# Running XOR over 67 million integers: six tile buffers instead of four, a merged carry path, and a descriptor cap

## Chip, cores, metric

One core of a Trainium2 chip. Times are device microseconds of that core. The kernel is a single program that is executed several times; medians are over those executions, and the profile is of one of them. A run counts as slow when it is over 1.5% above the fastest run of the same kernel; with one core this label rests on the time alone.

## The reference

```python
def setup_inputs():
    return {"x": np.random.randint(0, 256, (8192, 8192), dtype=np.int32)}

def reference(x):
    return np.bitwise_xor.accumulate(x.flatten()).reshape(x.shape)   # given back as int64
```

The kernel gets x as int64 and writes int64: 537 MB in and 537 MB out. As the values fit in 8 bits, it computes on the low 32-bit word of each element and leaves the high word alone.

## The kernel before

A tile is 128 partitions x 4096 elements of 8 bytes, 32,768 B a partition, 4 MB in all; 128 tiles. VectorE scans each partition with a tree of XORs in place, with strides. What carries from one partition to the next, and from one tile to the next, goes through TensorE: the 8 bits of each partition's total are multiplied by a triangular matrix of ones, and the lowest bit of each sum is the XOR.

```python
_F_CONFIGS = [(4096, (8, 8, 8, 8)), ...]
_NB = 4                                   # tile buffers
...
def front(i):                             # VectorE
    dve.wait_ge(sem_in[b], 16 * (i // NB + 1))     # the load has landed
    up_sweep(tb)                          # 28 XORs: 7 of 128x512, 7 of 128x64, 7 of 128x8, 7 of 128x1
    # mvi = total & 1<<k for 8 bits; mvf = mvi as float

def tail(i):
    dve.wait_ge(sem_pe, i + 1)
    # cint = psC as int; rint = cint & maskint; rfbuf = rint as float
    # ebuf = sum(rfbuf); tb[:, 0:1] = ebuf          (what this partition starts from)
    cd(lambda: dve.tensor_copy(c2int.ap(), psC2[0:1, q * _NMV : (q + 1) * _NMV]))
    cd(lambda: dve.tensor_tensor(gint.ap(), c2int.ap(), maskint[0:1, :], ALU.bitwise_and))
    cd(lambda: dve.tensor_copy(gmask[0:1, nq * _NMV : (nq + 1) * _NMV], gint.ap()))
    down_sweep(tb)                        # XORs of 8, 56, 448 and 3584 elements a partition

for i in range(T):
    front(i)
    if i > 0:
        tail(i - 1)
tail(T - 1)

# TensorE, tile i, after tail(i-1):
pe.matmul(psC[:, ...],    lmat,            mvf, start=True,  stop=False)
pe.matmul(psC[:, ...],    onesrow,         gmask, start=False, stop=True)
pe.matmul(psC2[0:1, ...], onescol,         mvf, start=True,  stop=False)   # one output row
pe.matmul(psC2[0:1, ...], onesrow[0:1,0:1], gmask, start=False, stop=True)

# SyncE issues the loads, ScalarE the stores:
if use > 0: sp.wait_ge(sem_out[b], 16 * use)      # the buffer's last store has landed
sp.dma_start(dst, src).then_inc(sem_in[b], 16)
...
act.wait_ge(sem_dve, dve_after_tail[i])
act.dma_start(dst, src).then_inc(sem_out[b], 16)
```

## Time and profile before

| | before |
|---|---|
| time, median of 4 runs | 2707.84 us (2706.84 to 2713.7) |
| span of the profiled run | 2705.8 us |
| VectorE (DVE) busy | 2347.6 us |
| 16 DMA engines, sum of both queues | 96.2% |
| moved | 1074 MB, 397 GB/s |
| VectorE waiting for loads | 148.3 us in 70 waits |

q1 is the load queue, q10 the store queue. The prediction shows these lines and reads them. Two more lines of the kernel before are needed later. First the page's chain that ended last, by engine, then the group of the widest strided sweep (columns: line, engine, operation, shapes, count | busy us, mean ns of one | idle us just before, and what ended it):

```profile
DMA 58%; DVE 39%; issue 2%; DVEq 0%; PE 0%
```

```profile
L156 DVE TENSOR_TENSOR tbuf<-tbuf 128x512 int32<-128x512 int32 x896 | 914.6, 1021 | 180.8 <-DMA tbuf<-in_x_dram 148.3
```

The first says that the end of the program follows from transfers more than from sweeps.

### The profile page before, as it was taken

What the parts mean: (1) busy time and instruction counts of PE and PEld (TensorE: products, weight loads), DVE (VectorE), ACT (ScalarE), POOL (GpSimd) and SP (SyncE); (2) the same over time, 40 slices, a digit from 0 to 9 for tenths busy, and PEclk for the clock granted to TensorE, in tenths of its full rate; (3) what the DMA queues carried; (4) which work ended last, traced back from release to release, by engine and by line L of the source; (5) the groups of instructions that cost most, each with busy time, mean ns of one, the idle gap of its engine ahead of it and who ended that gap; (6) DMA issues with size and microseconds to landing.
All of it is one profiled execution on the core that took longest, in us unless ns stands there. A gap on an engine that the chain in (4) does not pass through costs nothing.

```text
span 2705.8 us, 7983 instructions
## 1 busy us (share of the span) xinstructions
PE 174.7 (6%) x1024; PEld 149.1 (6%) x1024; DVE 2347.6 (87%) x5376; POOL 1.9 (0%) x17
## 2 busy tenths in 40 slices
PE   0000000000000000000000000000000000000000
PEld 0000000000000000000000000000000000000000
DVE  7988888888888888888888888888888888888886
POOL 0000000000000000000000000000000000000000
DMA  8999999999999999999999999999999999999997
GB/s 372 364 399 400 395 408 402 393 407 405 400 393 403 406 391 411 404 397 403 403 404 392 394 405 395 391 404 407 400 394 406 401 392 404 406 401 398 410 395 327
DMA packets 36919, 1074.27 MB, mean 397 GB/s; under 512 B 4097, under 2 KB 4097, under 8 KB 4097
## 3 DMA queue, kind: packets, MB, share of 16 engines
q1 hardware_dynamic: 18432, 536.88, 48.9%
q10 hardware_dynamic: 18432, 536.88, 47.3%
q14 instruction: 47, 0.38, 0.0%
q8 instruction: 8, 0.13, 0.0%
HBM read 536.87 MB, written 536.87 MB: 397 GB/s over the span
## 4 chain that ended last, share of the span: by engine, by line
DMA 58%; DVE 39%; issue 2%; DVEq 0%; PE 0%
DMA out_dram<-tbuf 29%; DMA tbuf<-in_x_dram 29%; DVE tbuf L156 24%; DVE tbuf L175 11%; DVE tbuf L166 0%; DVE mvf L196 0%; DVE rfbuf L218 0%; DVE mvi L188 0%; DVE rint L214 0%; DVE cint L209 0%; DVE ebuf L220 0%; DVE gmask L237 0%; DVE c2int L227 0%; DVE gint L232 0%; DVE tbuf L224 0%
## 5 line engine op out<-in xcount | busy, mean ns | idle before, releaser
L156 DVE TENSOR_TENSOR tbuf<-tbuf 128x512 int32<-128x512 int32 (+3 forms) x3584 | 1459.2, 407 | 273.4 <-DMA tbuf<-in_x_dram 148.3
L175 DVE TENSOR_TENSOR tbuf<-tbuf 128x56 int32<-128x56 int32 (+2 forms) x384 | 658.8, 1716 | 13.2
L257 PE MATMUL psC<-mvf,lmat 128*128 128x8 f32 x256 | 76.3, 372 | 2511.1 <-DVE tbuf L175 2485.2
L257 PEld LDWEIGHTS psC<-mvf,lmat 128*128 128x128 f32 x256 | 64.2, 312 | 2525.2 <-DVE tbuf L175 2499.4
L264 PE MATMUL psC<-gmask,onesrow 1*128 1x8 f32 x256 | 75.8, 367 | 0.0
L264 PEld LDWEIGHTS psC<-gmask,onesrow 1*128 1x128 f32 x256 | 63.7, 308 | 3.1
L209 DVE CAST cint<-psC 128x8 int32<-128x8 f32 x128 | 21.3, 166 | 14.5 <-PE psC L279 1.5
L166 DVE TENSOR_TENSOR tbuf<-tbuf 128x8 int32<-128x8 int32 x128 | 22.1, 173 | 4.4
L218 DVE CAST rfbuf<-rint 128x8 f32<-128x8 int32 x128 | 21.8, 170 | 4.4
L196 DVE CAST mvf<-mvi 128x8 f32<-128x8 int32 x128 | 21.9, 171 | 4.4
L188 DVE TENSOR_TENSOR mvi<-tbuf,maskint 128x8 int32<-128x8 int32 x128 | 21.4, 167 | 4.5
L271 PE MATMUL psC<-mvf,onescol 128*1 128x8 f32 x256 | 25.1, 172 | 0.0
L214 DVE TENSOR_TENSOR rint<-cint,maskint 128x8 int32<-128x8 int32 x128 | 21.3, 166 | 4.4
L279 PE MATMUL psC<-gmask,onesrow 1*1 1x8 f32 x256 | 24.6, 166 | 0.0
L220 DVE TENSOR_REDUCE ebuf<-rfbuf 128x1 f32<-128x8 f32 x128 | 20.6, 161 | 4.4
L237 DVE CAST gmask<-gint 1x8 f32<-1x8 int32 x128 | 20.2, 158 | 4.4
L227 DVE CAST c2int<-psC 1x8 int32<-1x8 f32 x128 | 19.8, 154 | 4.4
L232 DVE TENSOR_TENSOR gint<-c2int,maskint 1x8 int32<-1x8 int32 x128 | 19.7, 154 | 4.4
L224 DVE CAST tbuf<-ebuf 128x1 int32<-128x1 f32 x128 | 19.6, 153 | 4.5
L271 PEld LDWEIGHTS psC<-mvf,onescol 128*1 128x1 f32 x256 | 10.9, 81 | 3.1
L279 PEld LDWEIGHTS psC<-gmask,onesrow 1*1 1x1 f32 x256 | 10.3, 76 | 5.2
L127 POOL MEMSET maskint<- 128x1 int32 x8 | 0.8, 98 | 0.7 <-POOLq L324 0.3
(9 smaller groups left out, 1.3 us busy)
## 6 DMA issues: line engine op xcount, KB each, us to landing
tbuf<-in_x_dram SPq DMA_DIRECT2D x128, 4096.0 KB, 21.8
out_dram<-tbuf ACTq DMA_DIRECT2D x128, 4096.0 KB, 21.1
```

Of the source, the lines that this page charges most:

```text
L156: lambda o=o, i1=i1: dve.tensor_tensor(o, o, i1, ALU.bitwise_xor)
L166: cd(lambda: dve.tensor_tensor(ot, ot, it, ALU.bitwise_xor))
L175: lambda o=o, i1=i1: dve.tensor_tensor(o, o, i1, ALU.bitwise_xor)
L188: lambda: dve.tensor_tensor(mvi[:, q * _NMV : (q + 1) * _NMV], sb, maskint.ap(), ALU.bitwise_and,)
L196: lambda: dve.tensor_copy(mvf[:, q * _NMV : (q + 1) * _NMV], mvi[:, q * _NMV : (q + 1) * _NMV],)
L209: lambda: dve.tensor_copy(cint.ap(), psC[:, q * _NMV : (q + 1) * _NMV])
L214: lambda: dve.tensor_tensor(rint.ap(), cint.ap(), maskint.ap(), ALU.bitwise_and)
L218: cd(lambda: dve.tensor_copy(rfbuf.ap(), rint.ap()))
L257: pe.matmul(psC[:, q * _NMV : (q + 1) * _NMV], lmat.ap(), mvf[:, q * _NMV : (q + 1) * _NMV], start=True, stop=False,)
L264: pe.matmul(psC[:, q * _NMV : (q + 1) * _NMV], onesrow.ap(), gmask[0:1, q * _NMV : (q + 1) * _NMV], start=False, stop=True,)
L271: pe.matmul(psC2[0:1, q * _NMV : (q + 1) * _NMV], onescol.ap(), mvf[:, q * _NMV : (q + 1) * _NMV], start=True, stop=False,)
L279: lambda q=q: pe.matmul(psC2[0:1, q * _NMV : (q + 1) * _NMV], onesrow[0:1, 0:1], gmask[0:1, q * _NMV : (q + 1) * _NMV], start=False, stop= ...
```

## The change

Intent: more buffers, so that loads and stores run further ahead; one copy and one mask for both PSUM results instead of two of each; a cap on the length of a DMA descriptor.

```diff
-    (4096, (8, 8, 8, 8)),
+    (4096, (8, 8, 8, 8), 6),
...
-_NB = 4
+_MAX_DESC_BYTES = 32768
...
-                    dve.wait_ge(sem_pe, i + 1)
-                    cd(lambda: dve.tensor_copy(cint.ap(), psC[:, q * _NMV : (q + 1) * _NMV]))
+                    dve.wait_ge(sem_pe, 2 * (i + 1))
+                    cd(lambda: dve.tensor_copy(cint.ap(), psC[:, pqs]))          # 16 wide now
-                            rint.ap(), cint.ap(), maskint.ap(), ALU.bitwise_and
+                            rint.ap(), cint.ap(), mask16.ap(), ALU.bitwise_and
-                    cd(lambda: dve.tensor_copy(rfbuf.ap(), rint.ap()))
+                    cd(lambda: dve.tensor_copy(rfbuf.ap(), rint[:, 0:_NMV]))
...
-                    (copy of psC2 to c2int, mask of c2int to gint: both gone)
-                            gmask[0:1, nq * _NMV : (nq + 1) * _NMV], gint.ap()
+                            gmask[0:1, nq * _NMV : (nq + 1) * _NMV],
+                            rint[0:1, _NMV : 2 * _NMV],
...
-                        psC2[0:1, q * _NMV : (q + 1) * _NMV],   onescol.ap(),
+                        psC[:, c0 + _NMV : c0 + 2 * _NMV],      onesq.ap(),     # 128 output rows
-                            psC2[0:1, ...],  onesrow[0:1, 0:1],
+                            psC[:, c0 + _NMV : c0 + 2 * _NMV],  onesrow.ap(),
...
-                    sp.dma_start(dst, src).then_inc(sem_in[b], 16)
+                    sp.dma_start(dst, src, max_dma_last_dim=_MAX_DESC_BYTES).then_inc(sem_in[b], 16)
-                    act.dma_start(dst, src).then_inc(sem_out[b], 16)
+                    act.dma_start(dst, src, max_dma_last_dim=_MAX_DESC_BYTES).then_inc(sem_out[b], 16)
```

(The setup of the wider mask and of the square of ones is left out.)

More of the change, by code (lines that the diff above doesn't have):

```diff
@@ L10 @@
 _F_CONFIGS = [
-    (4096, (8, 8, 8, 8)),
-    (2048, (8, 8, 8, 4)),
-    (512, (8, 8, 8)),
-    (256, (4, 4, 4, 4)),
-    (64, (4, 4, 4)),
+    (4096, (8, 8, 8, 8), 6),
+    (2048, (8, 8, 8, 4), 4),
+    (512, (8, 8, 8), 4),
+    (256, (4, 4, 4, 4), 4),
+    (64, (4, 4, 4), 4),
 ]
-_NB = 4
 _NMV = 8
+_MAX_DESC_BYTES = 32768
 class _Chain:
@@ L55, in bass_scan_xor_kernel @@
         out32t = out.tensor
-    F = None
-    RADS = None
-    for f, rads in _F_CONFIGS:
-        if N % (P * f) == 0 and N // (P * f) >= 1:
-            F, RADS = f, rads
+    F = RADS = NB = None
+    for f, rads, nb in _F_CONFIGS:
+        if N % (P * f) == 0:
+            F, RADS, NB = f, rads, nb
             break
@@ L64, in bass_scan_xor_kernel @@
     T = N // (P * F)
-    NB = min(_NB, T)
+    NB = min(NB, T)
     L = len(RADS)
@@ L87, in bass_scan_xor_kernel @@
         ]
-        maskint = es.enter_context(nc.sbuf_tensor("maskint", [P, _NMV], DT.int32))
+        mask16 = es.enter_context(nc.sbuf_tensor("mask16", [P, 2 * _NMV], DT.int32))
         lmat = es.enter_context(nc.sbuf_tensor("lmat", [P, P], DT.float32))
+        onesq = es.enter_context(nc.sbuf_tensor("onesq", [P, P], DT.float32))
         onesrow = es.enter_context(nc.sbuf_tensor("onesrow", [1, P], DT.float32))
-        onescol = es.enter_context(nc.sbuf_tensor("onescol", [P, 1], DT.float32))
         gmask = es.enter_context(nc.sbuf_tensor("gmask", [1, 2 * _NMV], DT.float32))
@@ L94, in bass_scan_xor_kernel @@
         mvf = es.enter_context(nc.sbuf_tensor("mvf", [P, 2 * _NMV], DT.float32))
-        cint = es.enter_context(nc.sbuf_tensor("cint", [P, _NMV], DT.int32))
-        rint = es.enter_context(nc.sbuf_tensor("rint", [P, _NMV], DT.int32))
+        cint = es.enter_context(nc.sbuf_tensor("cint", [P, 2 * _NMV], DT.int32))
+        rint = es.enter_context(nc.sbuf_tensor("rint", [P, 2 * _NMV], DT.int32))
         rfbuf = es.enter_context(nc.sbuf_tensor("rfbuf", [P, _NMV], DT.float32))
         ebuf = es.enter_context(nc.sbuf_tensor("ebuf", [P, 1], DT.float32))
-        c2int = es.enter_context(nc.sbuf_tensor("c2int", [1, _NMV], DT.int32))
-        gint = es.enter_context(nc.sbuf_tensor("gint", [1, _NMV], DT.int32))
-        psC = es.enter_context(nc.psum_tensor("psC", [P, 2 * _NMV], DT.float32))
-        psC2 = es.enter_context(nc.psum_tensor("psC2", [P, 2 * _NMV], DT.float32))
+        psC = es.enter_context(nc.psum_tensor("psC", [P, 4 * _NMV], DT.float32))
         sem_pool = es.enter_context(nc.semaphore("c_pool"))
@@ L106, in bass_scan_xor_kernel @@
         sem_pe = es.enter_context(nc.semaphore("c_pe"))
-        sem_act = es.enter_context(nc.semaphore("c_act"))
-        sem_sp = es.enter_context(nc.semaphore("c_sp"))
         sem_in = [es.enter_context(nc.semaphore(f"in{b}")) for b in range(NB)]
@@ L126, in _ @@
                 for k in range(_NMV):
-                    cp(lambda k=k: pool.memset(maskint[:, k : k + 1], 1 << k))
+                    cp(lambda k=k: pool.memset(mask16[:, k : k + 1], 1 << k))
+                    cp(
+                        lambda k=k: pool.memset(
+                            mask16[:, _NMV + k : _NMV + k + 1], 1 << k
+                        )
+                    )
                 cp(lambda: pool.memset(onesrow.ap(), 1.0))
-                cp(lambda: pool.memset(onescol.ap(), 1.0))
+                cp(lambda: pool.memset(onesq.ap(), 1.0))
                 cp(lambda: pool.memset(gmask.ap(), 0.0))
@@ L190, in front @@
                             sb,
-                            maskint.ap(),
+                            mask16[:, 0:_NMV],
                             ALU.bitwise_and,
@@ L206, in tail @@
                     tb = tbufs[b]
-                    dve.wait_ge(sem_pe, i + 1)
-                    cd(
-                        lambda: dve.tensor_copy(
-                            cint.ap(), psC[:, q * _NMV : (q + 1) * _NMV]
-                        )
-                    )
-                    cd(
-                        lambda: dve.tensor_tensor(
-                            rint.ap(), cint.ap(), maskint.ap(), ALU.bitwise_and
-                        )
-                    )
-                    cd(lambda: dve.tensor_copy(rfbuf.ap(), rint.ap()))
+                    dve.wait_ge(sem_pe, 2 * (i + 1))
+                    pqs = slice(q * 2 * _NMV, (q + 1) * 2 * _NMV)
+                    cd(lambda: dve.tensor_copy(cint.ap(), psC[:, pqs]))
+                    cd(
+                        lambda: dve.tensor_tensor(
+                            rint.ap(), cint.ap(), mask16.ap(), ALU.bitwise_and
+                        )
+                    )
+                    cd(lambda: dve.tensor_copy(rfbuf.ap(), rint[:, 0:_NMV]))
                     cd(
@@ L227, in tail @@
                         lambda: dve.tensor_copy(
-                            c2int.ap(), psC2[0:1, q * _NMV : (q + 1) * _NMV]
-                        )
-                    )
-                    cd(
-                        lambda: dve.tensor_tensor(
-                            gint.ap(), c2int.ap(), maskint[0:1, :], ALU.bitwise_and
-                        )
-                    )
-                    cd(
-                        lambda: dve.tensor_copy(
-                            gmask[0:1, nq * _NMV : (nq + 1) * _NMV], gint.ap()
+                            gmask[0:1, nq * _NMV : (nq + 1) * _NMV],
+                            rint[0:1, _NMV : 2 * _NMV],
                         )
@@ L256, in _ @@
                     pe.wait_ge(sem_dve, need)
+                    c0 = q * 2 * _NMV
                     pe.matmul(
-                        psC[:, q * _NMV : (q + 1) * _NMV],
+                        psC[:, c0 : c0 + _NMV],
                         lmat.ap(),
@@ L263, in _ @@
                     )
-                    pe.matmul(
-                        psC[:, q * _NMV : (q + 1) * _NMV],
-                        onesrow.ap(),
-                        gmask[0:1, q * _NMV : (q + 1) * _NMV],
-                        start=False,
-                        stop=True,
+                    ce(
+                        lambda c0=c0, q=q: pe.matmul(
+                            psC[:, c0 : c0 + _NMV],
+                            onesrow.ap(),
+                            gmask[0:1, q * _NMV : (q + 1) * _NMV],
+                            start=False,
+                            stop=True,
+                        )
                     )
                     pe.matmul(
-                        psC2[0:1, q * _NMV : (q + 1) * _NMV],
-                        onescol.ap(),
+                        psC[:, c0 + _NMV : c0 + 2 * _NMV],
+                        onesq.ap(),
                         mvf[:, q * _NMV : (q + 1) * _NMV],
@@ L278, in _ @@
                     ce(
-                        lambda q=q: pe.matmul(
-                            psC2[0:1, q * _NMV : (q + 1) * _NMV],
-                            onesrow[0:1, 0:1],
+                        lambda c0=c0, q=q: pe.matmul(
+                            psC[:, c0 + _NMV : c0 + 2 * _NMV],
+                            onesrow.ap(),
                             gmask[0:1, q * _NMV : (q + 1) * _NMV],
@@ L296, in _ @@
                     dst = tbufs[b][:, W : W * (F + 1)]
-                    sp.dma_start(dst, src).then_inc(sem_in[b], 16)
+                    sp.dma_start(dst, src, max_dma_last_dim=_MAX_DESC_BYTES).then_inc(
+                        sem_in[b], 16
+                    )
             @block.scalar
@@ L305, in _ @@
                     src = tbufs[b][:, W : W * (F + 1)]
-                    act.dma_start(dst, src).then_inc(sem_out[b], 16)
+                    act.dma_start(dst, src, max_dma_last_dim=_MAX_DESC_BYTES).then_inc(
+                        sem_out[b], 16
+                    )
                 for b in range(NB):
```

## The prediction

> **What bounds the kernel now.** The kernel streams 128 tiles of 4 MB through four SBUF buffers. A tile is loaded, swept by VectorE (front), swept again one tile later (tail, behind the front of the next tile), and stored. I read the page's busy shares and DMA queues first, then the waits of VectorE and of the load queue, then the chain that ended last.
>
> Page, busy and queues:
>
> ```profile
> PE 174.7 (6%) x1024; PEld 149.1 (6%) x1024; DVE 2347.6 (87%) x5376; POOL 1.9 (0%) x17
> DMA packets 36919, 1074.27 MB, mean 397 GB/s; under 512 B 4097, under 2 KB 4097, under 8 KB 4097
> q1 hardware_dynamic: 18432, 536.88, 48.9%
> q10 hardware_dynamic: 18432, 536.88, 47.3%
> ```
>
> Two resources are nearly full: VectorE at 87%, the 16 DMA engines at 48.9 + 47.3 = 96.2%. Neither is at 100%, so neither alone explains 2705.8 us. The waits, first VectorE's, then the load queue's:
>
> ```profile
> DVE tbuf L156 <- DMA tbuf<-in_x_dram: 148.3, 70, 13.1
> DVE cint L209 <- PE psC L279: 1.5, 1, 1.5
> ...
> SPq L297 <- DMA out_dram<-tbuf: 2597.8, 124, 54.2
> ```
>
> VectorE waits for loads in 70 of 128 tiles; every load after the first four (124) waits for the store that frees its buffer. The chain of waits, one lap in the middle, columns start, duration, what:
>
> ```profile
> 1213.39 22.45 DMA out_dram<-tbuf
> 1235.85 23.53 DMA tbuf<-in_x_dram
> 1259.41 1.03 DVE tbuf L156
> ...
> 1275.29 3.90 DVE tbuf L175
> 1279.21 19.52 DMA out_dram<-tbuf
> ```
>
> The reader should see a loop: store of tile i, load of tile i+4 into the same buffer, front of i+4, tail of i+3, store of i+3. One lap advances three tiles. Its parts are in the page's DMA issues (last column: us to landing):
>
> ```profile
> tbuf<-in_x_dram SPq DMA_DIRECT2D x128, 4096.0 KB, 21.8
> out_dram<-tbuf ACTq DMA_DIRECT2D x128, 4096.0 KB, 21.1
> ```
>
> VectorE's share of a lap is one front and one tail. It worked from 13.1 to 2693.1 us; less the 148.3 - 13.1 = 135.2 of later load waits and the 1.5 for PE this is 2543.3 us, or 19.87 us a tile. The lap: 21.1 + 21.8 + 19.87 = 62.8 us for three tiles, 20.9 us a tile; 128 of these are 2679 us, and 13 at the start and 13 at the end make 2705. So the bound is **the round trip of a buffer**, with both engines a little below full.
>
> [...] the two queues' shares add to 96.2% and not above 100. [...] in the loads at the start (windows, last column GB/s):
>
> ```profile
> 10.00:20.00 10.00, 0.00 (x0) 0.00 (x0) 6.70 (x7) 0.00 (x0) 1.00 1.02 442
> 20.00:30.00 10.00, 1.34 (x8) 1.17 (x8) 9.00 (x28) 0.00 (x0) 1.00 0.97 419
> 30.00:40.00 10.00, 0.00 (x0) 0.00 (x0) 8.80 (x34) 0.00 (x0) 1.00 1.03 443
> ```
>
> [...] Trace: 3893 ns for N=3584[...], 166 for N=8[...]; the strided 128x512 ones take 1021[...], but they are unchanged. So for small operations the count matters, not the width. [...] six buffers of 32,776 B are 192.05 KiB and fit.
>
> **The change, part by part.**
>
> 1. Two VectorE operations a tile go: the copy of the second PSUM result and its mask. Forms, busy us and mean ns of one:
>
> ```profile
> L209 DVE CAST cint<-psC 128x8 int32<-128x8 f32 x128 | 21.3, 166 | 14.5 <-PE psC L279 1.5
> L227 DVE CAST c2int<-psC 1x8 int32<-1x8 f32 x128 | 19.8, 154 | 4.4
> L232 DVE TENSOR_TENSOR gint<-c2int,maskint 1x8 int32<-1x8 int32 x128 | 19.7, 154 | 4.4
> ```
>
> Each costs 0.154 busy plus 0.035 idle before it (4.4 us / 128): 0.189 us, two of them 0.378 us. The copy and mask that stay become 16 wide instead of 8[...]. Net -0.361 us a tile, 46 us in all: VectorE goes from 19.87 to 19.51 us a tile, 2497 us of work.
>
> 2. PE: the carry products become 128 rows wide. In the instruction order PE keeps four products a tile. A product pair of the wide kind takes 0.52 us start to start against 0.12 of the narrow, so PE's block grows from about 1.3 to 2.2 us. It begins at the end of a tail and is needed after a front of 12.3 us, so it is hidden except at the last tile: +0.8 us. PE's extra semaphore lies there too.
>
> 3. The descriptor cap of 32,768 bytes: a row is 4096 x 8 B = 32,768 B already, the built transfers of both kernels have the same shape (128 rows of 8192 words), and the packet records show 32,768 data packets of 32,768 B. Worth 0. So is the setup: eight more memsets of 0.1 us before the first load lands at 13.1 us.
>
> 4. Four buffers become six. The lap is then store i, load i+6, front i+6, tail i+5, store i+5: five tiles a lap. At today's durations (21.1 + 21.8 + 19.51)/5 = 12.5 us a tile. The loop stops being the bound; what remains is the larger of two capacities.
>
> VectorE capacity: 13.1 start + 2497 + 2.3 for the last PE wait + 12.7 for the last store (2693.1 to 2705.8) = 2525 us.
>
> DMA capacity: 256 data packets a tile over 16 engines are 16 in a row per engine, 2048 in all. The queue shares give 0.962 x 2705.8 / 2048 = 1.271 us a packet, so 2603 us even with no idle engine. But this mean is not the capacity. I sorted the trace's packet records by transfer: the median packet takes 1.213 us; the slow ones lie early in transfers that start on idle engines. Loads started after a gap beside an idle store queue average 1.378 us a packet (24 of them), beside a running store 1.249 (56); stores 1.305 (24) and 1.221 (76). With six buffers both queues nearly always hold work, so I take the second kind: (1.249 + 1.221)/2 = 1.235, and 1.25 as the careful figure: 2529 to 2560 us. To this add 1.8 us before the first packet and some 15 us of engines idling at the end (the trace has 11 us idle in a row at 2674, since the last tail follows the last load by a front and two tails): 2546 to 2577 us.
>
> So DMA becomes the bound by a little, 19.8 to 20.0 us a tile against VectorE's 19.5. [...] 2551 to 2582, and choose **2570 us**, 5% faster. Alone, part 1 would shorten the lap by 0.36/3 = 0.12 us a tile, 15 us; nearly all the gain is part 4.
>
> **The rivals.**
> (a) VectorE alone becomes the bound: 2525 to 2535 us. For: packets of 1.213 us, the median, would need only 2484 us. Against: even beside a running queue loads average 1.249.
> (b) DMA was the bound all along, and packets keep their 1.271 us because transfers' starts are slow however they begin: 2603 + 17 = 2620 us. For: 96.2% busy, and the 48 loads that followed directly on another load with the store queue idle averaged 1.296. Against: the second to fourth load at the start, back to back, ran at 1.213 to 1.219.
> (c) Mixed traffic slows down when reads and writes always overlap, so that a fuller queue just stretches packets: then 2650 to 2710 us, no gain. For: the mean of 397 GB/s is below the 419 to 443 of pure loads. Against: stores beside running loads had the shortest packets, 1.221.
>
> **Range and chances.** The low end is (a) plus a little, 2535; the high end is (b), 2620. I give 0.8 to that. The 2% line is 2707.84 x 0.98 = 2654 us, beyond (b), reached by (c) only, which I hold at 0.06. Slower needs extra packets or a broken overlap, which nothing here suggests: 0.01.
>
> **What would show it.** Right: VectorE's waits for loads remain, roughly 30 to 60 us with the start's 13; DMA shares sum to 98% or more with packets of 1.23 to 1.25 us; load and store landings lengthen to about (5 x 19.8 - 19.5)/2 = 40 us each on average[...]; L156 and L175 groups unchanged, two groups of 0.154 us gone, VectorE busy near 2347.6 - 39.5 + 2 = 2310 us. VectorE idle only between operations would show (a); packets at 1.27 would show (b), at 1.3 or more (c). The forecast is wrong if the chain still has laps of store, load, front and tail with idle DMA engines, or if the 128x512 sweeps lengthen beside denser transfers.

The net of 0.361 us a tile is 0.378 less 0.017 us for the two operations that become 16 wide (measured since: 174 and 175 ns, against 166). The DMA capacity came to 2546 to 2577 us; 5 us more, a guess of mine for what two engines with nearly the same time per tile cost each other, made 2551 to 2582, from which 2570 was chosen. What the trace of the kernel before shows for width: XORs of 1, 8 and 64 elements a partition took 159, 175 and 273 ns, the one of 3584 took 3893. That six buffers fit is shown by the runs that have six (e1 gave the right result).

## The result

| | before | after |
|---|---|---|
| median | 2708.18 us (15 runs, 2703.21 to 2713.7) | 2546.4 us (10 runs, 2546.16 to 2578.25) |
| span of the profiled run | 2705.8 us | 2544.8 us |
| VectorE busy | 2347.6 us | 2322.2 us |
| VectorE waiting for loads | 148.3 us in 70 waits | 13.3 us in 1 wait |

The ratio is 0.9422, 95% interval 0.9398 to 0.9446: the mean time of the fast runs of the one over that of the other in the same rounds, so not quite the ratio of the two medians. Eight of the ten runs lie within 0.5 us of each other; the other two took 2566.21 and 2578.25. Such outliers come back in the experiments.

The page of the changed kernel, busy and queues:

```profile
PE 277.1 (11%) x1024; PEld 255.7 (10%) x1024; DVE 2322.2 (91%) x5120; POOL 2.8 (0%) x25
DMA packets 36916, 1074.25 MB, mean 422 GB/s; under 512 B 4096, under 2 KB 4096, under 8 KB 4096
q1 hardware_dynamic: 18432, 536.88, 49.9%
q10 hardware_dynamic: 18432, 536.88, 49.5%
```

The DMA queues now add to 99.4%. By this line alone one would call DMA the bound. The waits of VectorE and of the load queue say otherwise:

```profile
DVE tbuf L156 <- DMA tbuf<-in_x_dram: 13.3, 1, 13.3
DVE cint L209 <- PE psC L270: 2.3, 1, 2.3
...
SPq L288 <- DMA out_dram<-tbuf: 2420.3, 122, 65.6
```

The single wait for a load is the first tile's. The load queue still waits for buffers, but no longer to anyone's cost. The chain agrees, first its shares on the page, then three pieces from its middle (start us, us, what):

```profile
DVE 93%; issue 5%; DMA 0%; DVEq 0%; PE 0%
```

```profile
1201.93 3.90 DVE tbuf L175
1205.93 1.12 DVE tbuf L156
1207.08 1.11 DVE tbuf L156
```

Where before it went store, load, sweep, it is now a tail's last XOR straight into the next front: VectorE sets the time. Its first two 128x512 sweeps take 1.12 and 1.11 us there. For the first that is nothing new: in tiles that don't wait for a load it takes 1.08 us in the mean in both kernels, and 1.03 in the lap that the prediction shows is that of a tile that waited. The second is new: 1.087 us in the mean against 1.017 before. The group as a whole, and the DMA issues (last column: median us from issue to landing):

```profile
L156 DVE TENSOR_TENSOR tbuf<-tbuf 128x512 int32<-128x512 int32 x896 | 926.3, 1034 | 53.0 <-DMA tbuf<-in_x_dram 13.3
```

```profile
tbuf<-in_x_dram SPq DMA_DIRECT2D x128, 4096.0 KB, 24.9
out_dram<-tbuf ACTq DMA_DIRECT2D x128, 4096.0 KB, 28.3
```

The sweep grew from 1021 to 1034 ns. The transfers take 53.2 us together, not the 80 (40 each) that the prediction expected with DMA as the bound. A lap of five tiles at VectorE's 19.66 us is 98.3 us; 53.2 in transfer and 19.7 in VectorE leave some 25 us in which a landed tile waits for VectorE. I call this waiting time the stock. The trace has both ends of it, the sixteenth increment of a load's semaphore and the start of the tile's first sweep: a mean of 29.9 us for tiles 8 to 15, 25.7 for tiles 60 to 67 and 13.9 for the last eight. So the loads came slightly more slowly than VectorE used them up in this run, and the program ended before the stock was gone.

### The profile page after: what moved, and what is told of

It reads as the page before. It is cut to its first block, busy times and chain, and to the rows that moved or that the text cites. A ratio compares the mean times of both kernels' runs of the same rounds, so it can differ in the third digit from the quotient of the medians.

```text
span 2544.8 us, 7736 instructions
## 1 busy us (share of the span) xinstructions
PE 277.1 (11%) x1024; PEld 255.7 (10%) x1024; DVE 2322.2 (91%) x5120; POOL 2.8 (0%) x25
## 3 DMA queue, kind: packets, MB, share of 16 engines
q1 hardware_dynamic: 18432, 536.88, 49.9%
q10 hardware_dynamic: 18432, 536.88, 49.5%
## 4 chain that ended last, share of the span: by engine, by line
DVE 93%; issue 5%; DMA 0%; DVEq 0%; PE 0%
DVE tbuf L156 59%; DVE tbuf L175 26%; DVE rint L211 1%; DVE cint L209 1%; DVE tbuf L166 1%; DVE mvf L196 1%; DVE rfbuf L215 1%; DVE mvi L188 1%; DVE ebuf L217 1%; DVE gmask L224 1%; DVE tbuf L221 1%; DMA tbuf<-in_x_dram 0%; DVEq L30 0%; PE psC L246 0%; PE psC L270 0%
## 5 line engine op out<-in xcount | busy, mean ns | idle before, releaser
L156 DVE TENSOR_TENSOR tbuf<-tbuf 128x512 int32<-128x512 int32 (+3 forms) x3584 | 1471.0, 410 | 145.6 <-DMA tbuf<-in_x_dram 13.3
L262 PE MATMUL psC<-mvf,onesq 128*128 128x8 f32 x256 | 76.2, 372 | 0.0
L254 PE MATMUL psC<-gmask,onesrow 1*128 1x8 f32 x256 | 75.8, 367 | 0.0
L270 PE MATMUL psC<-gmask,onesrow 1*128 1x8 f32 x256 | 75.8, 367 | 0.0
L262 PEld LDWEIGHTS psC<-mvf,onesq 128*128 128x128 f32 x256 | 64.1, 310 | 3.1
L254 PEld LDWEIGHTS psC<-gmask,onesrow 1*128 1x128 f32 x256 | 63.7, 308 | 3.1
L270 PEld LDWEIGHTS psC<-gmask,onesrow 1*128 1x128 f32 x256 | 63.7, 308 | 3.1
L209 DVE CAST cint<-psC 128x16 int32<-128x16 f32 x128 | 22.3, 174 | 16.1 <-PE psC L270 2.3
L211 DVE TENSOR_TENSOR rint<-cint,mask 128x16 int32<-128x16 int32 x128 | 22.3, 175 | 4.4
L188 DVE TENSOR_TENSOR mvi<-tbuf,mask 128x8 int32<-128x8 int32 x128 | 21.3, 167 | 4.5
L224 DVE CAST gmask<-rint 1x8 f32<-1x8 int32 x128 | 20.4, 159 | 4.4
L221 DVE CAST tbuf<-ebuf 128x1 int32<-128x1 f32 x128 | 19.6, 153 | 4.5
## 6 DMA issues: line engine op xcount, KB each, us to landing
tbuf<-in_x_dram SPq DMA_DIRECT2D x128, 4096.0 KB, 24.9
out_dram<-tbuf ACTq DMA_DIRECT2D x128, 4096.0 KB, 28.3
```

Source lines behind the costliest of these rows:

```text
L156: lambda o=o, i1=i1: dve.tensor_tensor(o, o, i1, ALU.bitwise_xor)
L188: lambda: dve.tensor_tensor(mvi[:, q * _NMV : (q + 1) * _NMV], sb, mask16[:, 0:_NMV], ALU.bitwise_and,)
L209: cd(lambda: dve.tensor_copy(cint.ap(), psC[:, pqs]))
L211: lambda: dve.tensor_tensor(rint.ap(), cint.ap(), mask16.ap(), ALU.bitwise_and)
L254: lambda c0=c0, q=q: pe.matmul(psC[:, c0 : c0 + _NMV], onesrow.ap(), gmask[0:1, q * _NMV : (q + 1) * _NMV], start=False, stop=True,)
L262: pe.matmul(psC[:, c0 + _NMV : c0 + 2 * _NMV], onesq.ap(), mvf[:, q * _NMV : (q + 1) * _NMV], start=True, stop=False,)
```

## The experiments

Twelve kernels were run, with four timed runs each. The runs of one group shared a chip and the runs of the kernel before, whose median was 2707.51, 2707.69 and 2708.3 us in the three groups. No kernel was refused; there is no e7.

| run | median us | all four runs |
|---|---|---|
| e1_buffers_only | 2584.94 | 2584.31 to 2585.12 |
| e2_four_buffers | 2699.96 | 2699.62 to 2701.71 |
| e3_five_buffers | 2547.44 | 2547.07 to 2547.92 |
| e4_no_cap | 2547.21 | 2547.07 to 2547.92 |
| e5_narrow_carry | 2557.66 | 2542.81, 2548.97, 2566.35, 2625.71 (slow) |
| e6_dma_only (wrong on purpose) | 2487.87 | 2487.21 to 2488.61 |
| e8_pe_later | 2601.94 | 2558.82, 2568.14, 2635.74 (slow), 2637.25 (slow) |
| e9_lean_pe_later | 2673.52 | 2550.7, 2672.04, 2675.0, 2680.84 (these three slow) |
| e10_dma_and_fetches (wrong on purpose) | 2544.84 | 2537.32, 2539.26, 2550.43, 2731.99 (slow) |
| e11_lean_paced | 2557.73 | 2557.18 to 2558.19 |
| e12_lean_five | 2577.36 | 2567.72 to 2582.81 |
| e13_pe_later_five | 2579.96 | 2572.8 to 2580.99 |

### e1: the buffers alone

```diff
 (kernel before)
-_NB = 4
+_NB = 6
```

> The kernel before with six buffers and nothing else. Theory V (in the changed kernel VectorE alone sets the time): its work per tile is that of the kernel before, 19.87 us by my count plus about 0.06 us of semaphore handling that the load waits hid, so 13.3 + 128 x 19.93 + 1.5 + 12.1 = 2578 us, no load waits after the first, and DMA queue shares that sum to about 98%. Theory D (DMA capacity sets the time of the changed kernel and VectorE merely keeps up): the same time as the changed kernel, 2546 us. Theory O (the removed operations matter and buffers do not): about 2700.

The 0.06 us of semaphore handling can be worked out from the kernel before: a front whose load has landed starts 0.105 us (median) after the tail, which 70 of 128 tiles hid behind a load wait, and 0.105 x 70/128 = 0.057. The copy that waits for TensorE starts 0.103 us after the operation before it, the operations that wait for no other engine 0.034 to 0.035.

Measured 2584.94 us, ratio 0.9547. VectorE's waits and the queues:

```profile
DVE tbuf L156 <- DMA tbuf<-in_x_dram: 13.4, 1, 13.4
```

```profile
q1 hardware_dynamic: 18432, 536.88, 49.9%
q10 hardware_dynamic: 18432, 536.88, 49.0%
```

Theory V holds, 7 us off: with six buffers VectorE's work is the time, and taking 0.3 us of it per tile (19.97 to 19.67, start to start of fronts) is worth 2584.94 - 2546.4 = 38.5 us. Note the queues' 98.9%: VectorE sets 19.97 us a tile, and DMA looks full at this pace, too. The busy share of the DMA engines cannot be read as distance from their capacity here: without sweeps the same transfers take 19.4 us a tile (e6).

### e2: everything but the buffers (with TensorE's wide products, and the cap, which e4 shows to be nothing)

```diff
 (changed kernel)
-    (4096, (8, 8, 8, 8), 6),
+    (4096, (8, 8, 8, 8), 4),
```

> The changed kernel with four buffers instead of six. Theory L (with four buffers the round trip over three tiles is the bound): 0.36 us less VectorE work per lap of three tiles is 15 us, so about 2692 us, with load waits still near 150 to 180 us. Rival V4 (VectorE time counts in full with four buffers too): 2708 - 46 = 2662 us.

```profile
DVE tbuf L156 <- DMA tbuf<-in_x_dram: 181.1, 85, 13.0
```

Measured 2699.96, ratio 0.9974: a gain of 7.5 us, not 15, and far from V4's 46. The work that was taken from VectorE came back as waiting, 148.3 to 181.1 us. The same edit is worth 7.5 us with four buffers and 38.5 with six: the parts do not add, and one has to be there before the other pays.

### e3: five buffers

```diff
-    (4096, (8, 8, 8, 8), 6),
+    (4096, (8, 8, 8, 8), 5),
```

> The changed kernel with five buffers. Theory R (reserve: the time between a load's landing and its sweep is a stock of about 32 us that six buffers build at the start and that DMA, a little slower per tile than VectorE, eats by 0.13 us a tile; five buffers hold one tile less, about 13 us): the stock is gone after some 100 tiles, VectorE then waits for loads, time 2550 to 2600 us and runs spread by more than 10 us. Rival L (round trip arithmetic: (21.1 + 21.8 + 19.66)/4 = 15.6 us a tile, well below VectorE's 19.66): no load waits, 2546 us.

```profile
DVE tbuf L156 <- DMA tbuf<-in_x_dram: 13.0, 1, 13.0
```

2547.44 us with no load waits and all runs within 0.9 us. My theory R, in which the stock is eaten at a fixed rate, is refuted as a rule: here the stock stays at 15.4, 13.4 and 15.3 us for the three groups of tiles. The lap arithmetic (rival L) was right: five buffers suffice.

### e4: no cap

```diff
-  sp.dma_start(dst, src, max_dma_last_dim=_MAX_DESC_BYTES)     (and the store likewise)
+  sp.dma_start(dst, src)
```

> The changed kernel without the descriptor cap. Expected: same packets (16,384 data packets of 32,768 bytes in each direction), same time, 2546 us, within the spread that the changed kernel itself shows (2546 to 2578). Rival: packets of another size and a time that differs by over 1%.

2547.21 us and 18,432 packets on each queue as with the cap: the cap does nothing, as rows are 32,768 bytes long without it. In this run the stock falls from 28.6 to 24.4 us and is still 23.6 at the end. The decline to 13.9 in the profiled run of the changed kernel is thus something that happens in some runs, or on some chips.

### e5: the carry product narrow again on TensorE

```diff
-                        psC[:, c0 + _NMV : c0 + 2 * _NMV],  onesq.ap(),
+                        psC[0:1, c0 + _NMV : c0 + 2 * _NMV],  onesq[:, 0:1],
-                            psC[:, c0 + _NMV : c0 + 2 * _NMV],  onesrow.ap(),
+                            psC[0:1, c0 + _NMV : c0 + 2 * _NMV],  onesrow[0:1, 0:1],
+                cd(lambda: dve.memset(psC.ap(), 0.0))      # once, at the start
```

> The changed kernel with the carry product narrow again on PE (one output row, as before; the PSUM area is zeroed once so that the wide copy reads defined data). Theory P (VectorE's 128x512 sweeps run longer while PE works, and the wide product makes PE's block cover two sweeps instead of one): the mean of the 128x512 group falls from 1034 to about 1021 ns and the time by 128 x 0.09 = 11.5 us to about 2535. Rival Q (the sweeps are longer because a store has just been issued): mean stays 1034, time 2546. Rival D (DMA sets the time): mean falls, but VectorE then waits for loads and the time stays within 3 us of 2546.

```profile
L157 DVE TENSOR_TENSOR tbuf<-tbuf 128x512 int32<-128x512 int32 x896 | 920.5, 1027 | 48.6 <-DMA tbuf<-in_x_dram 8.4 <-DVE tbuf L176 0.9
```

1027 ns, half way. By place in the front, the second of the seven sweeps fell from 1.087 to 1.024 us, as P says; the first stayed long (1.082 in the changed kernel, 1.096 here). The fastest run took 2542.81, 3.6 us below the changed kernel. But the runs now scatter from there to 2625.71, and in the profiled one the stock went from 28.6 to 4.1 us. By the ratio of fast runs (0.9428) nothing is gained.

### e8: TensorE's products later

```diff
                     need = dve_after_front[i] if i == 0 else dve_after_tail[i - 1]
+                    if 0 < i < T - 1:
+                        need += 15
```

> The changed kernel with PE's four products held back until VectorE is at the short 128x8 and 128x1 sweeps of the next front (PE waits for a count 15 operations higher, except for the first and last tile); the store's issue stays where it is. Theory P (PE's work lengthens the sweep beside it): 128x512 mean falls from 1034 to 1014 ns, some short sweeps lengthen or not. Rival Q (the store's issue lengthens it): mean stays near 1027 to 1034. Time: VectorE alone would give 2546 - 128 x 0.16 = 2526 us; Theory R (DMA is close behind): 2526 to 2560, with the landing-to-sweep stock down to nothing near the end and runs spread.

```profile
L156 DVE TENSOR_TENSOR tbuf<-tbuf 128x512 int32<-128x512 int32 x896 | 913.6, 1020 | 72.9 <-DMA tbuf<-in_x_dram 35.6
```

```profile
DVE tbuf L156 <- DMA tbuf<-in_x_dram: 35.6, 21, 13.2
```

The second sweep is at 1.015 us now, against 1.087 in the changed kernel: its lengthening belonged to TensorE's work beside it. The first is at 1.051 in the mean, in truth two kinds: over 1.06 us in 47 tiles, 1.015 in most others; in the changed kernel 106 of 128 are long. Rival Q, the store that is issued at that moment, is not enough to lengthen it: in the trace of e11 below, which also has the products moved, the store goes out 0.07 us before the first sweep just as in the changed kernel, and only 12 tiles are long. What lengthens the 47 here is open.

The short sweeps that the products now run beside did not suffer (128x8: 176 ns, before 175; 128x1: 159 in both). VectorE got quicker as planned, 19.57 us a tile while it does not wait, but the kernel did not: the two fast runs took 2558.82 and 2568.14. By fast runs alone the loss is not proven (0.9466, interval 0.9435 to 0.9496, against 0.9398 to 0.9446 for the changed kernel); e13 below decides it. The profiled one of these has no load waits until the stock is gone (28.1, 9.3, 0.0 us), and 20.07 us a tile over the last 40.

### e6: the transfers alone

```diff
-                for i in range(T):           # fronts and tails, TensorE
-                    ...
+                for i in range(T):
+                    dve.wait_ge(sem_in[b], 16 * (i // NB + 1))
+                    cd(lambda b=b: dve.memset(tbufs[b][:, 0:1], 0))
+                    dve_after_tail[i] = cd.count
```

> Wrong result on purpose: six buffers, the same loads and stores, no sweeps and no PE, only one small VectorE operation per tile that lets the store go. Theory N (DMA capacity is all but equal to VectorE's time): packets keep their mean of 1.234 us, so 2048 x 1.234 + 4 = 2531 us. Rival S (DMA has room, and only looked full because packets stretch into the time there is): packets at 1.213 us, 2488 us. Rival C (denser mixed traffic slows packets): above 2560 us.

```profile
DMA packets 36868, 1073.79 MB, mean 432 GB/s; under 512 B 4096, under 2 KB 4096, under 8 KB 4096
```

2487.87 us, on rival S to the microsecond. Loads and stores together ran at 432 GB/s, with mean packets of 1.215 and 1.213 us. So DMA by itself needs 19.4 us a tile, less than VectorE's 19.66, and mixing loads with stores costs nothing here (the second to fourth load of the kernel before, with no store beside them, ran at 1.213 to 1.219). The 1.234 us mean packet of the changed kernel is thus not the least that these transfers can have. What they need beside sweeps and instruction fetches is another question, which this run leaves open.

### e10: the same with instruction fetches

```diff
                     dve_after_tail[i] = cd.count
+                    for _ in range(40):
+                        cd(lambda: dve.memset(ebuf.ap(), 0.0))
```

> Wrong result on purpose: the DMA-only kernel with 40 tiny VectorE operations per tile added (6 to 7 us of otherwise idle VectorE time), so that as many instruction packets of 8 KB are fetched as in the changed kernel (about 44 of 309 ns) while the data traffic is unchanged. Theory F (all fetches fall on one of the 16 DMA engines, which then lags behind the other 15): 2488 + 40 x 0.309 = 2500 us, and the spread between the first and the last engine's landing of a transfer grows along the run. Rival G (fetches spread over the engines, or do not matter): 2488 to 2490 us, spread of 2 to 4 us as without them.

The page's instruction queue (packets, MB, share), of e6 and then of e10:

```profile
q14 instruction: 4, 0.03, 0.0%
```

```profile
q14 instruction: 44, 0.36, 0.0%
```

2537 to 2732 us. Theory F's 2500 is missed by far, but in the direction away from G. The spread between a load's first and last semaphore increment grew from 1.7 us (mean of the first eight loads) to 53 us (last eight); in e6 it stayed between 1.5 and 3.5. Forty 8 KB packets of 0.335 us in the mean (0.309 for the four of e6), 13 us in all, cannot take 50 us or more by their own length. Something turns a small disturbance into a lasting lag between engines: at tile 20 only the last of the sixteen increments is late (1.6 us from first to fifteenth, 7.0 to the last), at tile 124 eleven of the sixteen are, by 18 to 53 us. The run does not separate the fetches from the 5,120 small VectorE writes that come with them. That these writes hold the stores back is ruled out: a store is issued 0.15 to 0.22 us after its load has landed, as in e6.

### e9: one VectorE operation less

```diff
 (e8, and in the tail:)
-                    cd(lambda: dve.tensor_copy(rfbuf.ap(), rint[:, 0:_NMV]))
                     cd(lambda: dve.tensor_reduce(
-                            ebuf.ap(), rfbuf.ap(), mybir.AxisListType.X, ALU.add))
+                            ebuf.ap(), rint[:, 0:_NMV], mybir.AxisListType.X, ALU.add))
```

> The same, and VectorE sums the carry bits straight from the integers: one operation less per tile, 0.19 us, 25 us in all. Theory V (VectorE remains the bound): 2526 - 25 = 2501 us, no load waits. Theory R (DMA, with sweeps and stores as they are, needs about as much as VectorE now): the stock is used up before the middle, VectorE waits for loads again, and the time does not fall below 2520; it may even be above the changed kernel, with packets back at 1.25 us or more.

One run took 2550.7 us, three 2672 to 2681. The profile is of a slow one; its waits, issues and a lap of its chain:

```profile
DVE tbuf L156 <- DMA tbuf<-in_x_dram: 197.3, 87, 13.0
```

```profile
tbuf<-in_x_dram SPq DMA_DIRECT2D x128, 4096.0 KB, 42.5
out_dram<-tbuf ACTq DMA_DIRECT2D x128, 4096.0 KB, 45.0
```

```profile
1889.61 45.10 DMA out_dram<-tbuf
1934.72 42.66 DMA tbuf<-in_x_dram
```

The old loop is back, longer: (45.1 + 42.7 + 19.3)/5 = 21.4 us a tile, with six buffers. Why 45 us for a store? The trace keeps each of the sixteen increments of its semaphore. I read them as one per DMA engine, as the packet records have sixteen 4-byte writes per transfer, each behind eight data packets that follow one another; the trace doesn't number the engines. For the store of tile 100, us after its issue:

```
e1 (buffers only)   first 16.6   15th 17.3   16th 18.8
changed kernel      first 19.7   15th 26.6   16th 37.6
e9 (this run)       first 16.6   15th 17.3   16th 44.8
```

Fifteen engines finish in 17.3 us and one needs 44.8. Following that engine's packets back from one another, there is no gap between them: it works all the time, 16 data packets in 21.4 us, loads at 1.213 us and stores at 1.21 to 1.85, 1.44 in the mean, while the others finish, stop, and start again together. A buffer is free only when the last engine is through, so one late engine holds the whole loop.

### e11: the lean kernel slowed down

```diff
 (e9, before the down sweep:)
+                    for _ in range(2):
+                        cd(lambda: dve.tensor_copy(rfbuf.ap(), rint[:, 0:_NMV]))
```

> The lean kernel with PE later (VectorE 19.3 us a tile, median 2674 us), slowed down again on purpose by two idle copies of 0.19 us per tile. Theory M (nothing in that kernel is wrong but its pace: VectorE quicker than about 19.6 us a tile lets the DMA queues run into the slow pattern): VectorE 19.7 us a tile, no or few load waits, 2545 to 2560 us and runs close together, so slower VectorE, faster kernel. Rival W (holding PE back, or the direct sum, disturbs something else): still 2600 us or more.

```profile
DVE tbuf L156 <- DMA tbuf<-in_x_dram: 13.2, 1, 13.2
```

2557.18 to 2558.19 us, no load waits, and the stock rises from 30.0 to 35.4 us. Two useless operations a tile (19.77 us a tile) took away the slow pattern that three of e9's four runs were in. So the later TensorE and the direct sum are not enough to cause it; what differs is the pace. As this compares with slow runs of e9 (and on another chip), the next two, in which all runs are fast, carry the point.

### e12 and e13: the quick VectorE with five buffers

```diff
 (e9 and e8)
-    (4096, (8, 8, 8, 8), 6),
+    (4096, (8, 8, 8, 8), 5),
```

> The lean kernel with PE later and five buffers instead of six. Theory K (the lag of one DMA engine can only grow as far as buffers let the others run ahead; with five the slow pattern is milder): between 2510 and 2560 us, runs closer together than with six, landing spread under 10 us. Rival: less stock, so more load waits than with six: 2650 to 2700 us.

> The changed kernel with PE held back and five buffers. Theory K: 2524 to 2545 us, as VectorE's 19.5 us a tile allows, with runs close together, where six buffers gave 2559 to 2637. Rival: as with six or worse.

VectorE's load waits, e12 and then e13:

```profile
DVE tbuf L156 <- DMA tbuf<-in_x_dram: 88.6, 80, 13.3
```

```profile
DVE tbuf L156 <- DMA tbuf<-in_x_dram: 66.9, 63, 13.3
```

Theory K is half right. Runs lie together and no run is slow, and the lag is smaller. But both medians, 2577.36 and 2579.96, miss the ranges that I gave. Against e3, which has the same five buffers, a slower VectorE and 2547.44 us, e13 is 1.3% slower with all eight runs of the pair fast: making VectorE quicker cost 32 us. The two ran on different chips (e13 on that of e11, where the stock held with six buffers), on which the kernel before took 2707.69 and 2708.3 us; the ratios to it are 0.9407 (0.9392 to 0.9422) for e3 and 0.9523 (0.9506 to 0.9539) for e13. A slowed kernel with five buffers on e13's chip was not run.

The records of the profiled runs side by side, all in us: the stock as means over eight tiles; the spread between first and last increment of a store, mean of tiles 60 to 67; and the time from front to front over the last 40 tiles:

| | stock, tiles 8-15 | 60-67 | 120-127 | store spread | us a tile, late |
|---|---|---|---|---|---|
| changed kernel | 29.9 | 25.7 | 13.9 | 16.4 | 19.66 |
| e4 no cap | 28.6 | 24.4 | 23.6 | 14.3 | 19.67 |
| e3 five buffers | 15.4 | 13.4 | 15.3 | 5.3 | 19.67 |
| e5 narrow carry | 28.6 | 20.2 | 4.1 | 18.5 | 19.63 |
| e1 buffers only | 33.6 | 36.4 | 36.2 | 3.4 | 19.97 |
| e11 lean, paced | 30.0 | 35.5 | 35.4 | 3.0 | 19.77 |
| e13 PE later, five | 14.7 | 0.0 | 0.0 | 17.8 | 20.30 |
| e12 lean, five | 11.3 | 0.0 | 0.0 | 17.8 | 20.18 |
| e8 PE later | 28.1 | 9.3 | 0.0 | 25.5 | 20.07 |
| e9 lean (slow run) | 23.7 | 0.0 | 0.0 | 28.5 | 21.35 |

Where VectorE takes 19.77 or 19.97 us a tile, the stock holds and the DMA engines stay together. At 19.67 it holds, or nearly, in two profiled runs and shrinks in the third; at 19.63 (e5) it is all but gone at the end. Where VectorE is quicker (19.6 us in e8 and e13, 19.3 in e9 and e12, while it does not wait), the stock runs out, and then a tile costs more than it would at the slower pace. What makes the first engine fall behind, and why its stores stretch, is open. That the changed kernel's two runs of 2566 and 2578 us are runs in which the stock was used up fits the table, but none of them was profiled.

## Why the prediction was right, and where not

- **The bound before** (round trip of a buffer, 20.9 us a tile): right. e1 removes it with buffers alone and gains 122.6 us.
- **Part 4, six buffers**: right, and the largest part. The arithmetic of tiles per lap also holds for five (e3).
- **Part 3, the cap, worth 0**: right (e4).
- **Part 1, alone worth 15 us**: 7.5 (e2, which holds parts 2 and 3 too). The two operations that became 16 wide grew from 166 to 174 and 175 ns, 0.017 us together. "Nearly all the gain is part 4" is right for the parts alone, but with six buffers part 1 is worth 38.5 us, near the 46 that its operations were counted at.
- **"So DMA becomes the bound by a little"**: this step failed. VectorE sets the time (chain 93% DVE, no load waits after the first), which was rival (a). The failed term is the capacity of DMA, 1.235 to 1.25 us a packet: measured alone it is 1.213 to 1.215, 2488 us in all (e6). I took means of packets in a kernel that starves its DMA, and even the chosen ones beside a running queue may have held some of that. How far off the term is in the changed kernel stays open: with as many instruction fetches and small VectorE writes, but no sweeps, the transfers took 2537 to 2550 us in the fast runs (e10), near the 2546 to 2577 of the prediction. What refutes the step is that the profiled run of the changed kernel never waited for a load after the first. The forecast that landings would be 40 us each failed with it: 24.9 and 28.3.
- **VectorE's capacity, 2525 us** in rival (a): the span is 2544.8. Two terms were left out. The 128x512 sweeps grew by 926.3 - 914.6 = 11.7 us, and the idle time before L156 apart from load waits grew from 273.4 - 148.3 = 125.1 to 145.6 - 13.3 = 132.3, 7.2 us, since a front whose load has landed still starts 0.105 us (median, both kernels) after the tail, which in 70 tiles counted as load wait before. 2525.4 + 11.7 + 7.2 = 2544.3.
- **Part 2, TensorE "hidden except at the last tile"**: hidden as a wait, yes, and the last one is 2.3 us. But it lengthens the sweep that runs beside it (second sweep 1.087 us; 1.024 with the narrow product, 1.015 with TensorE moved away). The second sweep is 9.0 of the 11.7 us. The other 2.7 are the first sweep, which is no longer than before in tiles that don't wait (1.083 and 1.082 us; the first product is wide in both kernels), but was 1.044 in the 70 that waited.
- **The time**: 2570 forecast, 2546.4 measured, inside 2535 to 2620. The wrong bound cost 24 us, and the missing terms of the right bound made its own figure 20 us too low; had I chosen (a), the range of 2525 to 2535 would have been missed. That 2546.4 lies in the wide range is partly luck: one number too high and another too low enclosed it.
- **The signs that it named**: shares of 98% or more (99.4), packets of 1.23 to 1.25 us (1.234) and two groups gone came true although DMA was not the bound, so the first two tell nothing. Load waits of 30 to 60 us (13.3), landings of 40 us and unchanged L156 sweeps did not, and the sign of (a), VectorE idle only between operations, did. The sweeps did lengthen, which it had named as a sign of being wrong, but mostly from TensorE's products (9.0 of the 11.7 us) and not from denser transfers: the third to seventh sweeps take 1.013 to 1.014 us in both kernels.
- **Time against width**: the prediction names 3893 ns for the XOR with N=3584 and 166 for an operation with N=8. Other XORs and masks with N=8 took 154 to 175 ns.
- **The 5 us for two engines that cost each other time** (my guess): fails worse than any other term once VectorE is quicker. With a stock that is used up, a tile takes 0.4 to 1.7 us more than the changed kernel's 19.66 (table, late tiles), not 5 us in all.

No experiment gave a version that is reliably faster than the changed kernel. e5 has a run below it (2542.81) and e9 one just above (2550.7), and both scatter.

## What to carry to other kernels

Count tiles per lap of the buffer loop: here it told how many buffers are enough (five, e3), and an edit off that loop paid little while the loop was the bound (7.5 against 38.5 us for the same edit). A DMA share of 99% said nothing of the room left (98.9% at 19.97 us a tile in e1, and 19.4 us in e6); run the transfers alone to learn it, and take that as the best case (2488 us alone, 2537 and more with fetches and small VectorE writes beside them). When two engines are as close as here (19.4 us a tile for the transfers alone, 19.66 for VectorE), look at the stock between them and at each engine's landing, not only at means, and time several runs: here a quicker VectorE made a slower kernel.
